# The feed-forward block of a fused transformer kernel: order of the second half's units, w2's sums taken of w2 times g2, another order of the passes, layer norms in pairs

## The chip, the cores and the metric

The kernel runs on one core of a Trainium2 chip. The metric is the device time of one execution in microseconds (us). The core has a matrix engine (PE, whose weight loads have a row of their own, PEld), a vector engine (DVE), an activation engine (ACT), a general engine (POOL) and a queue from which all transfers are issued (SP). Each of them takes its instructions strictly in order and waits at the first one whose inputs or buffers are not ready.

## The reference

A block with differential attention, a gated linear recurrence and a SwiGLU feed-forward layer over 2048 tokens of width 1024, in float32. The change lies in the last part alone:

```python
x = layer_norm(ALPHA * x + g1 * y, ln1_g, ln1_b)
h = modulate(layer_norm(x), sh2, sc2)
a, b = split(h @ w1)                  # w1: 1024 x 2*2816
f = (silu(a) * b) @ w2                # w2: 2816 x 1024
x = layer_norm(ALPHA * x + g2 * f, ln2_g, ln2_b)
```

Here g2 is a vector over the 1024 output columns; it comes from the conditioning vector and is known early.

## The kernel before

A float32 product is made of three products of split numbers: each operand is kept as a rounded part and a rest, and `mm3` issues high times high, high times low and low times high (lines 151 to 153). The split is a cast on ACT and a subtraction, mostly on DVE.

Both products of the feed-forward layer are cut into 2x2 blocks and computed with Strassen's scheme in Winograd's form: seven passes in place of eight, on sums of blocks. S1 to S4 are the sums of the left operand's blocks A11 to A22, T1 to T4 those of the right operand's blocks B11 to B22; `OPS` names the two operands of each pass.

**First product (lines 1040 to 1400).** A `Unit(tb, j)` computes one 128-wide chunk j (of 22) of the hidden layer for two of the four token blocks: group tb=0 is blocks 0 and 1, tb=1 is blocks 2 and 3. It has seven passes of 12 matmuls. For each pass `prep` splits a piece of w1; the sums of w1's blocks are made on POOL (lines 1062 to 1067) out of tiles that SP loads. `fin` takes each pass's sum out of PSUM, mostly on DVE; line 1122 is one addition on POOL in each unit. `put` stores the hidden tile to `hid_d`. The 44 units run in the order tb=0, j=0 to 21, then tb=1, j=0 to 21. Split pieces of w1 rotate over 11 buffers, in the last two units over 7; PSUM has 8 banks.

Two further things are made beside the units:

- The left sums of the second product. They need A11, A12 (group 0, j below 11 and from 11 on) and A21, A22 (group 1, likewise). As soon as `put` has a hidden tile of group 1 with j of 11 or more, it loads three tiles (`qA`), makes S1 and S3 on POOL (lines 1087, 1088) and S2 and S4 on DVE (1089, 1090), and stores four tiles to `sum_d` (`S_d` in the trace). That falls in the last 11 units.
- The right sums, `w2_sums(j)` for j=0 to 10: four loads of w2, four operations on POOL (lines 1373 to 1376), four stores to `t_d` (`T_d`). They are written after units 6 to 16.

Both take their tiles from one pool, `qp`, with six buffers that are used in rotation.

**Second product (lines 1400 to 1525).** Seven passes of eight token tiles each; step n = 8*pass + i. Each step has 33 matmuls and reads a left tile that `load_hid` has loaded and split (line 1431: pieces m=0, 1, 2 on DVE or POOL), and the pass's right operand, which `prep_w2` loads and splits ahead (lines 1413, 1414). The order of the passes is 1, 2, 6, 7, 5, 3, 4. Output tile ti (of 16) has two halves of 512 columns; half 0 of tiles 0 to 7 is complete after pass 2, half 1 of tiles 8 to 15 after pass 5, half 1 of tiles 0 to 7 after pass 3, half 0 of tiles 8 to 15 after pass 4. `evict` adds the PSUM bank to the accumulators, and for a complete half `final` follows on DVE:

```python
V.tensor_tensor(o, o, g2b[:, c], ALU.mult)                       # L1460
V.scalar_tensor_tensor(y, y, ALPHA, o, ALU.mult, ALU.add)        # L1461
V.bn_stats(stt[:, ti, hf, :], y)                                 # L1462
```

A tile's first half is stored to `y0_d`. With its second half the whole layer norm follows at once: the statistics and seven small instructions for the root, two scalings on ACT (L1475), two multiplications by `lg` on POOL (L1476), two additions of `lb` (L1477, one on DVE, one on POOL), two stores. So the norms of tiles 0 to 7 lie in the sixth pass and those of tiles 8 to 15 in the seventh.

What sets the order: a scheduler takes the program in the order in which it is written, and moves instructions on each engine ahead of others by times that it assumes. On the chip that order is fixed.

Of the kernel before, what the change touches and what calls it, by code (L numbers as in the profile page):

```python
# [19 lines left out]
P = 128  # L20
D = 1024
# [29 lines left out]
PASSES = ((1, "A11", "B11"), (2, "A12", "B21"), (6, "S2", "T2"), (7, "S3", "T3"), (5, "S1", "T1"), (3, "S4", "B22"),  # L51
# [14 lines left out]
def kernel(ctx: ExitStack, tc: tile.TileContext, x, cx, prm_d, wa1, wa2, b_ada, w_in, w_v, lqk,  # L66
# [7 lines left out]
    def dma(o, i):  # L74
# [16 lines left out]
           for n in ("T1", "T2", "T3", "T4")}  # L91
    hid_d = [dram.tile([4, P, NJ, P], F32, tag=f"hid{b}", name=f"hid_d{b}") for b in range(NB)]
    y0_d = [dram.tile([P, 512], F32, tag=f"y0{i}", name=f"y0_d{i}") for i in range(16)]
# [950 lines left out]
    class Unit:  # L1044
# [29 lines left out]
        def put(self, s, o):  # L1074
            col = lambda d, j: d[:, :, j, :].rearrange("i p t -> p i t")
            row = lambda t: t.rearrange("p (i t) -> p i t", t=P)
            dma(col(hid_d[2 * self.tb + s], self.j), row(o))
            j = self.j - NJ // 2
            if self.tb == 0 or j < 0:
                return  # L1080

            a = {}
            for n, (b, jj) in (("A21", (2 + s, j)), ("A11", (s, j)), ("A12", (s, self.j))):
                a[n] = qp.tile([P, 512], F32, tag="q", name="q" + n)
                dma(row(a[n]), col(hid_d[b], jj))
            s1 = qp.tile([P, 512], F32, tag="q", name="qS1")
            G.tensor_tensor(s1, a["A21"], o, ALU.add)  # L1087
            G.tensor_tensor(a["A21"], a["A11"], a["A21"], ALU.subtract)  # L1088
            V.tensor_tensor(a["A11"], s1, a["A11"], ALU.subtract)
            V.tensor_tensor(a["A12"], a["A12"], a["A11"], ALU.subtract)  # L1090
            for n, t in (("S1", s1), ("S3", a["A21"]), ("S2", a["A11"]), ("S4", a["A12"])):
                dma(col(sum_d[n][s], j), row(t))

# [76 lines left out]
    units = [Unit(tb, j) for tb in range(2) for j in range(NJ)]  # L1170
# [193 lines left out]
    ahead(2)  # L1364
    def w2_sums(j):

        q = {}
# [12 lines left out]
    for n, u in enumerate(units[6:NJ - 1]):  # L1380
        whole(u, std)
        if n < NJ // 2:
            w2_sums(n)
# [32 lines left out]
    def load_hid(n, q):  # L1416
# [8 lines left out]
        for r in range(2 - q):  # L1425
# [5 lines left out]
            (G if m == 1 or (m == 0 and p > 4) else V).tensor_tensor(t[:, 1], raw[:, 4 * r:4 * r + w],  # L1431
# [14 lines left out]
    g2b = lnp.tile([P, D], F32, tag="g2b", name="g2b")  # L1446
# [139 lines left out]
```

## Time and profile before

| | us |
|---|---|
| Time, median of 3 runs | 2931.16 (2929.72 to 2933.06) |
| The profiled execution's own time | 2931.16 |
| Its span from the first to the last instruction | 2929.3 |
| First product, roughly | 1560 to 2460 |
| Second product, first to last matmul | 2460 to 2894 |
| After the last matmul | 35.3 |

Times within the span are counted from its start. The profile gives for each engine how long it was busy, and for each instruction what released it where the engine had been idle. A matmul of the two products starts every 0.226 us when nothing holds it, 443 in 100 us, so that a stretch with fewer shows how much PE lost there. The granted clock of PE is 1.00 (2.4 GHz) in most stretches and 0.5 (1.2 GHz) for some us after a long pause.

### The profile page before, as it was taken

How to read it: one execution, taken by the hardware profiler on the slowest of the kernel's cores; microseconds unless marked ns; L12 is line 12 of the kernel's file. 1: busy time of each engine (PE TensorE's matmuls, PEld its weight loads, DVE VectorE, ACT ScalarE, POOL GpSimd, SP SyncE). 2: the span in 40 equal slices, each digit the busy share in tenths (PEclk: the TensorE clock that was granted, in tenths of full speed). 3: DMA queues.
4: the chain of work that ended last, by engine and by line, in shares of the span. 5: the costliest groups of instructions: out<-in, count | busy, mean ns of one | idle time of the engine just before them, and what ended most of it. 6: DMA issues, size and time to landing. Idle time of an engine off the chain costs nothing. (4 is left out here: it accounts for less than half of the span.)

```text
span 2929.3 us, 37944 instructions
## 1 busy us (share of the span) xinstructions
PE 2728.2 (93%) x13188; PEld 2270.8 (78%) x13188; DVE 2140.4 (73%) x3399; ACT 1431.0 (49%) x2056; POOL 1559.1 (53%) x1019
## 2 busy tenths in 40 slices
PE   8889889878999999999999899999999988999994
PEld 4868767767899999987777787887888876888873
DVE  7754796596898999995888866758656657544688
ACT  3546668653677777774235433334333223433332
POOL 2004544454788888871454788445545655211376
PEclk9999999989999999999999999999999999999997
DMA  8875537357132322217463476333324888855543
GB/s 326 305 232 175 200 107 273 121 182 221 38 76 76 76 69 60 65 62 255 137 236 109 159 236 218 101 87 91 112 86 123 246 253 273 272 161 167 193 170 128
DMA packets 328848, 474.32 MB, mean 162 GB/s; under 512 B 26056, under 2 KB 201288, under 8 KB 326096
## 3 DMA queue, kind: packets, MB, share of 16 engines
q1 hardware_dynamic: 328656, 471.90, 50.0%
q8 instruction: 104, 1.70, 0.2%
q14 instruction: 88, 0.72, 0.1%
HBM read 313.46 MB, written 158.35 MB: 161 GB/s over the span
## 5 line engine op out<-in xcount | busy, mean ns | idle before, releaser
L857 DVE TENSOR_SCALAR_CACHE_REDUCE e<-ps_s 128x768 f32<-128x768 f32 x384 | 359.5, 951 | 37.3 <-PE ps_s L855 30.0
L873 POOL TENSOR_TENSOR a<-e,e 128x768 f32<-128x768 f32 x192 | 349.3, 1848 | 18.5 <-PE pt L936 13.8
L855 PE MATMUL ps_s<-k,q 128*128 128x384 f32 x1536 | 336.7, 351 | 13.2 <-DVE e L857 11.9
L862 ACT ACTIVATE e<-e,nm 128x2304 f32<-128x2304 f32 x128 | 285.4, 2229 | 52.3 <-DVE nm L861 49.2
L855 PEld LDWEIGHTS ps_s<-k,q 128*128 128x128 f32 x1536 | 268.7, 192 | 28.4 <-DVE e L857 21.4
L1431 POOL TENSOR_TENSOR hid<-hf,hid 128x512 fp32r<-128x512 f32 x72 | 100.4, 1396 | 245.1 <-ACT hid L1430 240.2
L940 ACT CAST ah<-pt 128x512 fp32r<-128x512 f32 x288 | 165.9, 582 | 130.0 <-PE pt L936 127.2
L941 DVE TENSOR_TENSOR al<-pt,ah 128x512 fp32r<-128x512 f32 x288 | 195.9, 686 | 36.1 <-ACT ah L940 35.7
L870 POOL TENSOR_SCALAR e<-e,rr,rn 128x2304 f32<-128x2304 f32 x64 | 146.6, 2291 | 90.2 <-DVE nm L861 48.9
L1062 POOL TENSOR_TENSOR s<-w1r 128x512 f32<-128x512 f32 x44 | 59.5, 1353 | 226.8 <-DMA w1r<-in_w 204.0
L151 PE MATMUL ps_p<-ht,w 128*128 128x512 f32 (+1 forms) x416 | 162.9, 392 | 16.6 <-DVE kf L213 11.6
L936 PE MATMUL pt<-ident,a 128*128 128x128 f32 x1152 | 175.3, 275 | 3.0 <-POOL a L873 2.8
L936 PEld LDWEIGHTS pt<-ident,a 128*128 128x128 f32 x1152 | 144.8, 142 | 42.8 <-POOL a L873 3.7
L153 PE MATMUL ps_p<-ht,w 128*128 128x512 f32 (+1 forms) x416 | 162.2, 392 | 6.6 <-DVE w L183 6.5
L1430 ACT CAST hid<-hf 128x512 fp32r<-128x512 f32 x168 | 95.7, 582 | 148.3 <-PE ps L153 133.1
L152 PE MATMUL ps_p<-ht,w 128*128 128x512 f32 (+1 forms) x416 | 162.3, 390 | 0.0
L219 POOL TENSOR_TENSOR lo<-kf,hi 128x512 fp32r<-128x512 f32 (+1 forms) x36 | 58.8, 1635 | 177.5 <-ACT hi L218 140.6
L929 PE MATMUL po<-ah,v 128*128 128x512 f32 x288 | 126.7, 440 | 0.6 <-ACT ah L940 0.6
L1122 POOL TENSOR_TENSOR v<-v,q 128x512 f32<-128x512 f32 x44 | 68.1, 1549 | 99.4 <-DVE u L1121 99.4
L930 PE MATMUL po<-al,v 128*128 128x512 f32 x288 | 116.8, 405 | 3.1 <-DVE al L941 1.4
L931 PE MATMUL po<-ah,v 128*128 128x512 f32 x288 | 114.7, 398 | 0.0
L151 PEld LDWEIGHTS ps_p<-ht,w 128*128 128x128 f32 x416 | 80.6, 194 | 36.1 <-issue 12.2
(3365 smaller groups left out, 8493.7 us busy)
## 6 DMA issues: line engine op xcount, KB each, us to landing
w1r<-in_w SPq DMA_DIRECT2D x88, 512.0 KB, 4.1
hid_d<-hid SPq DMA_DIRECT2D x88, 256.0 KB, 2.7
qA<-hid_d SPq DMA_DIRECT2D x66, 256.0 KB, 3.7
S_d<-qA SPq DMA_DIRECT2D x66, 256.0 KB, 5.9
wraw<-in_w_in SPq DMA_DIRECT2D x32, 512.0 KB, 4.6
adaw<-in_wa SPq DMA_DIRECT2D x32, 512.0 KB, 4.7
q<-q_d SPq DMA_DIRECT2D x64, 256.0 KB, 4.8
oy<-oy_d SPq DMA_DIRECT2D x16, 1024.0 KB, 5.8
```

The source lines that it names most:

```text
L151: PE.matmul(ps, lhsT=lh, rhs=rh, start=start, stop=False)
L152: PE.matmul(ps, lhsT=lh, rhs=rl, start=False, stop=False)
L153: last["pe"] = PE.matmul(ps, lhsT=ll, rhs=rh, start=False, stop=stop).ins
L855: PE.matmul(ps[:, j, :384], lhsT=q[:, m, part, qt * P:(qt + 1) * P], rhs=kst[h, m][:, c0:c0 + 384], start=(part == 0), stop=(part == 1))
L857: V.tensor_scalar(et[:, cc * 768:(cc + 1) * 768].rearrange("p (a b) -> p a b", a=2), ps[:, :, :384], -0.125, None, ALU.mult, ALU.min, accu ...
L862: S.activation(et, et, AF.Exp, bias=nm[:, m:m + 1], scale=-1.0, accum_out=ss[m])
L870: G.tensor_scalar(es[1], es[1], rr, rn, ALU.mult, ALU.mult)
L873: last["a"] = G.tensor_tensor(a, es[0][:, g * 768:(g + 1) * 768], es[1][:, g * 768:(g + 1) * 768], ALU.add).ins
L929: PE.matmul(po, lhsT=vh, rhs=ah, start=(j == 0), stop=False)
L936: PE.transpose(pt[:, qt * P:(qt + 1) * P], ath[h, b, qt, j // 6][:, (j % 6) * P:(j % 6 + 1) * P], ident)
L940: S.copy(ah, pt)
L941: V.tensor_tensor(al, pt, ah.bitcast(F32), ALU.subtract)
```

## The change

1. The units of the second group run in pairs: j=0, 11, 1, 12, and so on. `put` makes S3 (now as A11 - A21) when the tile of the first half is there, and S1, S2, S4 at the second half's tile: four loads and four stores for each j and block in place of three and four, spread over 22 units in place of 11. S1 and S2 are on POOL, S3 and S4 on DVE. S1, S2 and S3 overwrite tiles that were loaded, so that a put takes one or three buffers in place of four.
2. `g2_row` makes g2 as a row on all partitions and stores it to `g2_d`. `w2_sums(j)` is written after units 10 to 20; it loads two tiles of g2 as well, multiplies the four tiles of w2 by them on DVE, stores three of the products (`B11`, `B22`, `B21`) and makes the four sums as before on POOL. So it has six loads, four DVE and four POOL operations and seven stores, and takes seven buffers of the six in rotation. `prep_w2` always reads from `t_d`, and L1460 is gone.
3. The passes run 1, 2, 6, 5, 3, 7, 4: tiles 0 to 7 are complete after the fifth pass, half 1 of tiles 8 to 15 after the sixth, half 0 after the seventh.
4. `final` stores every half (but one) to `y_d`. `complete` does the norm later, for two tiles at once with one root, from halves that it loads again: tiles 0 to 7 at steps 35, 39, 43 and 47, tiles 8 to 14 at steps 50, 52 and 54, and tile 15 at the end with four fused operations on DVE. From the fifth pass on (before: the sixth) POOL makes piece m=0 of line 1431 too.

```diff
-PASSES = ((1, "A11", "B11"), (2, "A12", "B21"), (6, "S2", "T2"), (7, "S3", "T3"), (5, "S1", "T1"), (3, "S4", "B22"),
+PASSES = ((1, "A11", "B11"), (2, "A12", "B21"), (6, "S2", "T2"), (5, "S1", "T1"), (3, "S4", "B22"), (7, "S3", "T3"),
...
-            j = self.j - NJ // 2
-            if self.tb == 0 or j < 0:
+            if self.tb == 0:
                 return
...
+            a11 = load("A11", hid_d[s], j)
+            if j == self.j:
+                V.tensor_tensor(a11, a11, o, ALU.subtract)
+                return store("S3", a11)
+            a21, a12 = load("A21", hid_d[2 + s], j), load("A12", hid_d[s], self.j)
+            G.tensor_tensor(a21, a21, o, ALU.add)
+            store("S1", a21)
+            G.tensor_tensor(a11, a21, a11, ALU.subtract)
+            store("S2", a11)
+            V.tensor_tensor(a12, a12, a11, ALU.subtract)
+            store("S4", a12)
...
-    units = [Unit(tb, j) for tb in range(2) for j in range(NJ)]
+    units = [Unit(0, j) for j in range(NJ)] + [Unit(1, j + h * (NJ // 2)) for j in range(NJ // 2) for h in range(2)]
...
+        for c in range(2):
+            g.append(qp.tile([P, 512], F32, tag="q", name="g2"))
+            dma(g[c], g2_d[:, c * 512:(c + 1) * 512])
         for n, (r, c) in (("B11", (0, 0)), ("B12", (0, 1)), ("B22", (1, 1)), ("B21", (1, 0))):
...
             dma(q[n], w2[jj * P:(jj + 1) * P, c * 512:(c + 1) * 512])
+            V.tensor_tensor(q[n], q[n], g[c], ALU.mult)
+            if n != "B12":
+                dma(t_d[n][j], q[n])
+        G.tensor_tensor(q["B11"], q["B12"], q["B11"], ALU.subtract)
         t2 = qp.tile([P, 512], F32, tag="q", name="wT2")
-        G.tensor_tensor(q["B11"], q["B12"], q["B11"], ALU.subtract)
...
-            (G if m == 1 or (m == 0 and p > 4) else V).tensor_tensor(t[:, 1], raw[:, 4 * r:4 * r + w],
+            (G if m == 1 or (m == 0 and p > 3) else V).tensor_tensor(t[:, 1], raw[:, 4 * r:4 * r + w],
...
-        V.tensor_tensor(o, o, g2b[:, c], ALU.mult)
         V.scalar_tensor_tensor(y, y, ALPHA, o, ALU.mult, ALU.add)
         V.bn_stats(stt[:, ti, hf, :], y)
...
+        dma(y_d[ti][:, hf], y)
+
+    def complete(tis, y=None):
...
+                if ti == 15:
+                    V.scalar_tensor_tensor(t, t, mv[:, 0, k:k + 1], lg[:, c], ALU.subtract, ALU.mult)
+                    V.scalar_tensor_tensor(t, t, rs[:, k:k + 1], lb[:, c], ALU.mult, ALU.add)
+                else:
+                    S.activation(t, t, AF.Identity, bias=nb[:, k:k + 1], scale=rs[:, k:k + 1])
+                    G.tensor_tensor(t, t, lg[:, c], ALU.mult)
+                    (G if hf else V).tensor_tensor(t, t, lb[:, c], ALU.add)
...
+    norms = {35: (0, 1), 39: (2, 3), 43: (4, 5), 47: (6, 7), 50: (8, 9), 52: (10, 11), 54: (12, 13, 14)}
```

The order on PE is the same as before. On SP, in the middle of w2's sums, there stands before, from one store of T4 to the next (w1r is a load of w1, hid_d a store of a hidden tile):

```order
L75 DMA T4_d2_131<-wB21_16606 128x512
L75 DMA wB21_16766<-in_w2 128x512
L75 DMA w1r_16472<-in_w1 128x1024
L75 DMA T1_d3_99<-wB11_16760 128x512
L75 DMA T2_d3_110<-wT2_16768 128x512
L75 DMA wB11_16920<-in_w2 128x512
L75 DMA T3_d3_121<-wB12_16762 128x512
L75 DMA wB12_16922<-in_w2 128x512
L75 DMA wB22_16924<-in_w2 128x512
L75 DMA T4_d3_132<-wB21_16766 128x512
```

Now, from the store of T4 of j=3 on:

```order
L75 DMA T4_d3_165<-wB21_17426 128x512
L75 DMA wB12_17590<-in_w2 128x512
L75 DMA wB22_17593<-in_w2 128x512
L75 DMA wB21_17597<-in_w2 128x512
L75 DMA B11_d4_100<-wB11_17586 128x512
L75 DMA w1r_16770<-in_w1 128x1024
L75 DMA B22_d4_122<-wB22_17593 128x512
L75 DMA B21_d4_111<-wB21_17597 128x512
L75 DMA T1_d4_133<-wB11_17586 128x512
L75 DMA g2_17753<-g2_d_173 128x512
L75 DMA T2_d4_144<-wT2_17602 128x512
L75 DMA g2_17755<-g2_d_173 128x512
```

The loads of g2 and the stores of B11, B22 and B21 have come in. From the first T4 to the last (ten sums) there stood 11 loads of w1, two to a unit, and now there stand 15.

On POOL, in the last units of the first product, there stands before (s are sums of w1, v and q the units' own additions, qS and qA the left sums):

```order
L1087 TENSOR_TENSOR qS_20619<-qA_20613,hid 128x512
L1088 TENSOR_TENSOR qA_20613<-qA_20615,qA_20613 128x512
L1062 TENSOR_TENSOR s_20877<-w1r 128x512
L1063 TENSOR_TENSOR s_20878<-s_20877,w1r 128x512
L1087 TENSOR_TENSOR qS_20655<-qA_20649,hid 128x512
L1088 TENSOR_TENSOR qA_20649<-qA_20651,qA_20649 128x512
L1122 TENSOR_TENSOR v<-v,q 128x512
L1067 TENSOR_TENSOR s_20878<-w1r,s_20878 128x512
L1123 TENSOR_TENSOR q<-u,q 128x512
L1065 TENSOR_TENSOR s_20877<-w1r 128x512
```

Now, over one unit without left sums and the beginning of the next one with them:

```order
L1063 TENSOR_TENSOR s_19906<-w1r 128x512
L1064 TENSOR_TENSOR s_19907<-s_19906,w1r 128x512
L1132 TENSOR_TENSOR v<-v,q 128x512
L1068 TENSOR_TENSOR s_19907<-w1r,s_19907 128x512
L1133 TENSOR_TENSOR q<-u,q 128x512
L1066 TENSOR_TENSOR s_19906<-w1r 128x512
L1097 TENSOR_TENSOR qA_19823<-qA_19823,hid 128x512
L1099 TENSOR_TENSOR qA_19821<-qA_19823,qA_19821 128x512
L1097 TENSOR_TENSOR qA_19856<-qA_19856,hid 128x512
L1099 TENSOR_TENSOR qA_19854<-qA_19856,qA_19854 128x512
L1063 TENSOR_TENSOR s_20057<-w1r 128x512
L1064 TENSOR_TENSOR s_20058<-s_20057,w1r 128x512
```

Each unit had four operations for the left sums; now every second one has four.

On DVE, at the last two output tiles, there stands before (f takes the PSUM bank, mv to nb are the norm's statistics and root):

```order
L1500 TENSOR_TENSOR f_25858<-acc,ps 128x512
L1460 TENSOR_TENSOR f_25858<-f_25858,g2b 128x512
L1461 SCALAR_TENSOR_TENSOR y<-y,f_25858 128x512
L1477 TENSOR_TENSOR y<-y,lb_22282 128x512
L1462 BN_STATS stt<-y 128x6
L1469 BN_AGGR mv_25867<-stt 128x2
L132 TENSOR_SCALAR rs_a<-mv_25867 128x1
L134 RECIPROCAL rs_y<-rs_y 128x1
L135 TENSOR_TENSOR rs_t<-rs_a,rs_y 128x1
L136 TENSOR_TENSOR rs_t<-rs_t,rs_y 128x1
```

Now, from the last bank's f on:

```order
L1524 TENSOR_TENSOR f_25965<-acc,ps 128x512
L1506 TENSOR_TENSOR y_25919<-y_25919,lb_22470 128x512
L1477 SCALAR_TENSOR_TENSOR y<-y,f_25965 128x512
L1478 BN_STATS stt<-y 128x6
L1488 BN_AGGR mv<-stt 128x2
L133 TENSOR_SCALAR rs_a<-mv 128x1
L1501 SCALAR_TENSOR_TENSOR y<-y,mv,lg_22469 128x512
L1501 SCALAR_TENSOR_TENSOR y_25988<-y_25988,mv,lg_22469 128x512
L135 RECIPROCAL rs_y<-rs_y 128x1
L136 TENSOR_TENSOR rs_t<-rs_a,rs_y 128x1
L137 TENSOR_TENSOR rs_t<-rs_t,rs_y 128x1
L138 TENSOR_SCALAR rs_t<-rs_t 128x1
```

The addition of `lb` to tile 14 (y_25919) now stands between the last bank's f and its scaled addition, and the multiplication by `lg` of the last tile has come before the root.

## Rows read from the trace of the kernel before

**Rows 1.** The page's head: span and instructions.

```profile
span 2929.3 us, 37944 instructions
```

**Rows 2.** Windows: stretch, PE, PEld, DVE, ACT, POOL busy (count), clock, DMA, GB/s.

```profile
1667.00:1802.00 135.00, 129.98 (x574) 106.54 (x573) 93.10 (x88) 41.31 (x74) 123.14 (x82) 1.00 0.77 252
1740.00:1820.00 80.00, 74.64 (x325) 60.35 (x324) 53.94 (x54) 23.45 (x43) 71.47 (x48) 1.00 0.72 241
1860.00:1960.00 100.00, 100.00 (x443) 82.79 (x442) 63.52 (x78) 35.16 (x59) 44.77 (x32) 1.00 0.31 90
2370.00:2470.00 100.00, 81.08 (x329) 62.79 (x328) 65.07 (x82) 28.64 (x53) 51.43 (x37) 0.93 0.89 268
...
2818.00:2842.00 24.00, 17.06 (x59) 12.71 (x58) 21.30 (x36) 9.63 (x18) 16.84 (x12) 0.79 0.52 173
2842.00:2894.00 52.00, 49.81 (x218) 40.28 (x216) 44.97 (x72) 15.44 (x30) 41.68 (x28) 1.00 0.45 155
```

**Rows 3.** PE's longest wait, 2380 to 2520: us in total, times, longest.

```profile
PE ps L153 <- DVE w__21783 L1072: 6.7, 1, 6.7
```

**Rows 4.** Timeline of the longest wait: start, us, operation, [idle before <-releaser].

```profile
2409.81 1.26 POOL L1087 TENSOR_TENSOR qS<-qA,hid 128x512 f32<-128x512 f32 x1 [8.45 <-DMA S_d<-qA]
...
2413.55 1.73 DVE L1089 TENSOR_TENSOR qA<-qS,qA 128x512 f32<-128x512 f32 x1 [8.93 <-POOL qA L1088]
...
2415.80 0.67 DVE L1072 TENSOR_TENSOR w__21783<-w1r,w__21783 128x512 fp32r<-128x512 f32 x1
...
2416.53 0.79 PE L153 MATMUL ps<-B,w__21783 128*128 128x512 f32 x1 [6.71 <-DVE w__21783 L1072]
```

**Rows 5.** Windows of L1122 alone (one per unit): stretch, busy (count), clock, DMA.

```profile
1671.00:1809.00 138.00, 8.22 (x6) 1.00 0.76 249
2107.00:2240.00 133.00, 11.98 (x7) 1.00 0.29 83
2262.00:2416.00 154.00, 10.91 (x7) 0.99 0.86 246
```

**Rows 6.** Transfers 1667 to 1802: count, size, median us to landing.

```profile
wB<-in_w SPq DMA_DIRECT2D x44, 256.0 KB, 4.4
T_d<-wB SPq DMA_DIRECT2D x32, 256.0 KB, 4.5
```

**Rows 7.** Groups of the second product: count, busy us, mean ns, idle before.

```profile
L1461 DVE SCALAR_TENSOR_TENSOR y<-y,f 128x512 f32<-128x512 f32 x32 | 38.7, 1208 | 0.7
L1431 DVE TENSOR_TENSOR hid<-hf,hid 128x384 fp32r<-128x384 f32 x56 | 37.0, 663 | 14.9 <-ACT hid L1430 14.9
...
L1460 DVE TENSOR_TENSOR f<-f,g2b 128x512 f32<-128x512 f32 x32 | 25.2, 788 | 0.4
L1475 ACT ACTIVATE y<-y,nb,rs_y 128x512 f32<-128x512 f32 x32 | 24.3, 808 | 26.2 <-DVE nb L1472 23.7 <-DMA out<-y 2.5
L1462 DVE BATCH_NORM_STATS2 stt<-y 128x6 f32<-128x512 f32 x32 | 22.0, 688 | 0.5
...
L1495 DVE TENSOR_TENSOR f<-ps,acc 128x512 f32<-128x512 f32 x16 | 11.0, 685 | 16.9 <-PE ps L153 16.9
```

**Rows 8.** Timeline of POOL over one tile of the seventh pass.

```profile
2880.21 3.06 POOL L1476 TENSOR_TENSOR y<-y,lg 128x512 f32<-128x512 f32 x2 [1.18 <-ACT y L1475]
...
2889.91 3.07 POOL L1476 TENSOR_TENSOR y<-y,lg 128x512 f32<-128x512 f32 x2 [1.19 <-ACT y L1475]
```

**Rows 9.** Timeline of the end: the last matmul, and DVE's last additions.

```profile
2893.63 0.39 PE L153 MATMUL ps<-w__25210,hid 128*128 128x512 f32 x1
...
2917.87 1.74 DVE L1477 TENSOR_TENSOR y<-y,lb 128x512 f32<-128x512 f32 x1 [1.15 <-POOL y L1476]
...
2924.41 1.63 DVE L1477 TENSOR_TENSOR y<-y,lb 128x512 f32<-128x512 f32 x1
```

**Rows 10.** Transfers of the output halves in the second product: median us to landing.

```profile
y_d<-y SPq DMA_DIRECT2D x16, 256.0 KB, 2.7
...
y<-y_d SPq DMA_DIRECT2D x13, 256.0 KB, 3.1
```

More of the change, by code (lines that the diff above doesn't have):

```diff
@@ L90 @@
     t_d = {n: [dram.tile([P, 512], F32, tag=f"{n}{j}", name=f"{n}_d{j}") for j in range(NJ // 2)]
-           for n in ("T1", "T2", "T3", "T4")}
+           for n in ("B11", "B21", "B22", "T1", "T2", "T3", "T4")}
+    g2_d = dram.tile([P, D], F32, tag="g2", name="g2_d")
     hid_d = [dram.tile([4, P, NJ, P], F32, tag=f"hid{b}", name=f"hid_d{b}") for b in range(NB)]
-    y0_d = [dram.tile([P, 512], F32, tag=f"y0{i}", name=f"y0_d{i}") for i in range(16)]
+    y_d = [dram.tile([P, 2, 512], F32, tag=f"y{i}", name=f"y_d{i}") for i in range(16)]
     wo_d = [dram.tile([P, 2, D], F32R, tag=f"wo{k}", name=f"wo_d{k}") for k in range(8)]
@@ L1077, in put, with load, store @@
             dma(col(hid_d[2 * self.tb + s], self.j), row(o))
-            j = self.j - NJ // 2
-            if self.tb == 0 or j < 0:
+            if self.tb == 0:
                 return
[L1082 to L1091, printed above, removed]
-                dma(col(sum_d[n][s], j), row(t))
+            j = self.j % (NJ // 2)
+            def load(n, d, j):
+                t = qp.tile([P, 512], F32, tag="q", name="q" + n)
+                dma(row(t), col(d, j))
+                return t
+            def store(n, t):
+                dma(col(sum_d[n][s], j), row(t))
+            a11 = load("A11", hid_d[s], j)
[9 more added lines that the diff above has]
+            store("S4", a12)
         def mms(self, p, ks, first, last_):
@@ L1378, in w2_sums @@
             dma(t_d[n][j], t)
-    for n, u in enumerate(units[6:NJ - 1]):
+    for u in units[6:10]:
         whole(u, std)
-        if n < NJ // 2:
-            w2_sums(n)
+    g2_row()
+    for n, u in enumerate(units[10:NJ - 1]):
+        whole(u, std)
+        w2_sums(n)
     sliced(units[NJ - 1], std, range(4), lambda k: build(1, k))
@@ L1473, in final @@
-        for a, t in ((1 - hf, y0), (hf, y)):
-            ca = slice(a * 512, (a + 1) * 512)
-            S.activation(t, t, AF.Identity, bias=nb, scale=rs)
-            (V if ti == 15 else G).tensor_tensor(t, t, lg[:, ca], ALU.mult)
-            (V if a == hf else G).tensor_tensor(t, t, lb[:, ca], ALU.add)
-            dma(out[ti * P:(ti + 1) * P, ca], t)
+        if ti == 15 and hf == 0:
+            return y
+        dma(y_d[ti][:, hf], y)
+    def complete(tis, y=None):
+        mv = sm.tile([P, 2, 4], F32, tag="mv", name="mv", bufs=4)
+        n = len(tis)
+        for k, ti in enumerate(tis):
+            V.bn_aggr(mv[:, :, k], stt[:, ti])
+        rs = rsqrt(mv[:, 1, :n], n, LN_EPS)
+        nb = sm.tile([P, 2], F32, tag="nb2", name="nb2")[:, :n]
+        V.scalar_tensor_tensor(nb, mv[:, 0, :n], -1.0, rs, ALU.mult, ALU.mult)
+        for k, ti in enumerate(tis):
+            for hf in range(2):
+                c = slice(hf * 512, (hf + 1) * 512)
+                if y is None or hf:
+                    t = tile2("y5")
+                    dma(t, y_d[ti][:, hf])
+                else:
+                    t = y
+                if ti == 15:
+                    V.scalar_tensor_tensor(t, t, mv[:, 0, k:k + 1], lg[:, c], ALU.subtract, ALU.mult)
+                    V.scalar_tensor_tensor(t, t, rs[:, k:k + 1], lb[:, c], ALU.mult, ALU.add)
+                else:
+                    S.activation(t, t, AF.Identity, bias=nb[:, k:k + 1], scale=rs[:, k:k + 1])
+                    G.tensor_tensor(t, t, lg[:, c], ALU.mult)
+                    (G if hf else V).tensor_tensor(t, t, lb[:, c], ALU.add)
+                dma(out[ti * P:(ti + 1) * P, c], t)
@@ L1489, in evict @@
             V.tensor_tensor(u, ps, u, ALU.add)
[L1490 removed]
+        elif num == 5:
             V.tensor_tensor(t, ps, u, ALU.add)
@@ L1520 @@
                     mm3(ps, h[:, 0, j % 4], h[:, 1, j % 4], w[:, 0], w[:, 1], j == 0, j == HJ - 1)
-        evict(PASSES[p][0], i, pss[n])
+        y = evict(PASSES[p][0], i, pss[n])
+        if n in norms:
+            complete(norms[n][:2])
+            for ti in norms[n][2:]:
+                complete([ti])
+    complete([15], y)
     s5.close()
```

52 lines of the change are left out of this document (17 added, 35 removed).

## The prediction

> **What bounds the kernel now.** I read four views in this order: the windows, for the stretches in which PE does not run at its pace; PE's waits there; the timeline around the longest of them; and the timeline of the end. The sum is made against the profiled execution, whose span is 2929.3 us [rows 1]; its own time, 2931.16 us, is also the median of the three runs, so 1.9 us are added at the end.
>
> In the feed-forward layer PE is the bound wherever nothing goes wrong: 443 matmuls in 100 us, one in 0.226 us [rows 2]. A unit of 84 matmuls then takes 19.0 us, a step of 33 takes 7.45 us. A stretch's loss is the count that is missing at that pace (some per cent of records can be missing from a trace, so I take a us off in mind, not in the sum). There are four losses that the change can touch:
> - 1740 to 1820, beside w2's sums: 325 matmuls for 354, 6.6 us [rows 2].
> - 2370 to 2470, the end of the first product: 329 for 443, 25.7 us [rows 2].
> - 2818 to 2842: 59 for 106, 10.7 us; 2842 to 2894: 218 for 230, 2.8 us; together 13.5 us [rows 2].
> - After the last matmul, which ends at 2894.0, the span goes on for 35.3 us [rows 1, 9].
>
> The second of these is a chain: PE waits 6.7 us for a split piece of w1 [rows 3], and much the same once more a unit later; that piece waits on DVE behind S2, which waits 8.9 us for POOL, which has itself stood 8.5 us at S1, waiting for the tile that was loaded into a buffer of the ring after a store [rows 4]. The cause lies earlier. POOL's one addition per unit comes every 133/7 = 19.0 us in a quiet stretch, but every 154/7 = 22.0 us when the left sums are made, with transfers at a share of 0.86 in place of 0.29 [rows 5]. DVE and POOL fall 3 us behind in each of 11 units, and PE lives on its lead until it is used up.
>
> **The left sums (part 1 of the change).** The work per j and block rises from seven transfers to eight, POOL's and DVE's operations stay at two each. But it is spread over 22 units in place of 11: eight transfers per unit in place of 14. So the left sums took 0.57 of the transfers' time; 8/14 of that gives 0.29 + 0.33 = 0.62. POOL has two such operations per unit in place of four. With a third of the transfers' time free and little over half the buffers' traffic, I see no reason for the 3 us per unit to go on. The put's transfers are still issued on SP among w1's loads, so a wait there can still hold a load, and the last two units still have few buffers for split pieces: of the 25.7 us I leave 5.7 and take **-20**. Bounds: -25 (nothing left) and -5 (the in-order waits on loaded tiles matter more than the share).
>
> **w2's sums (part 2).** Three things are added. Four DVE multiplications per j, 44 in all: the trace of before has no such operation there; the nearest is a DVE operation of the same stretch, 93.1/88 = 1.06 us [rows 2], so 4.2 us per j. Five more transfers per j. And a longer ring, which I think decides. The six buffers now serve seven tiles, and T4 is made in the place of B21, whose store must have left first. So from one T4 store to the next there lie, one after the other: T4's store (4.5), the load of the next B21 (4.4), its multiplication (1.06), the store of B21 (4.5), the operation for T4 on POOL, 123.1/82 = 1.5 us [rows 2, 6]. That is 16.0 us; with 1.2 us for turns in three queues (an estimate, less than one operation in each) **17.2 us per j**. SP's order has 15 loads of w1, 7.5 units, over ten such cycles: 142 us at PE's pace against 172. So DVE and POOL fall 30 us behind. DVE's own work there, 14 operations per unit before and 5.3 more, is 19.3 x 1.06 = 20.5 us per unit, less than the 22.9 that the ring gives, so the ring is the later of the two.
>
> How much of that reaches PE is read from before: six units took 138 us in place of 114 [rows 5], 24 us late, and PE lost 6.6 of them; the lead covers 17.4 us. So PE loses 30 - 17.4 = 12.1 us with unrounded figures, 5.5 more than before: **+5.5**. Bounds: -6.6, if the cycle stays under 14.2 us and nothing is lost, and +28 at 19.5 us per j. Behind a DVE that waits for a tile of w2 stand the evictions of PSUM and the splits of w1; behind an SP that waits for a store stand the loads of w1. That is how it gets to PE.
>
> The Trainium skill speaks against this term (DMA: Bandwidth & Descriptors, section "Anatomy of one DMA — SWDGE (gpsimd) path"): a transfer costs about 2.0 us plus its bytes at 436 GB/s. By that an estimate for 256 KB is 2.6 us, the cycle would be 11.6 us and nothing would be lost; the transfers of this stretch took 4.4 and 4.5 us [rows 6], so the rule's price is not met here.
>
> The row of g2 itself is six transfers and two POOL operations once, off PE's path behind the lead. The sums now end later, but seven units before the second group's right operands are built; at 19 us a unit the lag is made up by then. I cost both at nothing; if that cover is gone, the build's loss grows by a few us, which is inside the upper bound.
>
> **The second product (parts 2 to 4).** Removed from DVE: 32 multiplications of 0.79 us [rows 7], which lay in all output passes, and seven of 16 roots. But where nothing was late, that is worth nothing: PE runs at 443 in 100 us until the sixth pass. What is late there is POOL. In the last two passes each tile has two multiplications, one addition and two splits on POOL, and a tile takes 9.7 us, from 2880.21 to 2889.91, where PE needs 7.45 [rows 8]. Sixteen tiles give 16 x 2.25 = 36 us that PE's lead, PE's stall (13.5) and the tail must take.
>
> Now the sixteen norms lie over the last three passes, eight of them in 16 steps. Per four steps of the fifth and sixth pass POOL has eight splits and six operations of a norm: 14 x 1.5 = 21 us of 29.8. DVE has per step of the sixth pass two sums from PSUM (0.69 each), the scaled addition (1.21), statistics (0.69) and a split (0.66) [rows 7], 15.7 us in four steps; two additions of `lb`, 3.5 [rows 9]; a root, 1.7 (what the 4.8 us from 2919.6 to 2924.4 leave beside statistics, a scaling of 0.81 and two multiplications of 0.79) [rows 7, 9]; and 5.5 splits of w2 at the 1.06 from above, 5.8: 26.7 us of 29.8. In the seventh pass POOL has 14 splits and 21 operations, 53 us of 59.6. Close, but below. Of the 13.5 us I leave 2: **-11.5**. Bounds: -13.5 and 0.
>
> **The end.** The last norm no longer waits behind a tile that is 9.7 us long. But the fixed order on DVE puts the addition of `lb` to tile 14 before the last tile's scaled addition, and tile 14 has to go out and come back first. Count from the last matmul's end, T. Tile 14's step ends at T - 7.45; an addition of `lb` with its wait for POOL (1.15 + 1.74) [rows 9], the sum (0.69) and the scaled addition (1.21) [rows 7] follow: T - 2.7. Store 2.7 and load 3.1 [rows 10]: T + 3.1. ACT 0.81, POOL 1.53 [rows 7, 8], the addition of `lb` 1.74: T + 7.2. Then tile 15: scaled addition 1.21, statistics 0.69, two fused operations like it (2.42), the root 1.7, two more (2.42): T + 15.6. From DVE's last end, 2926.0, to the span's end there are 3.3 us [rows 1, 9]. So 18.9 us in place of 35.3: **-16.5**. Bounds: -24 (tile 14 in time, so that T + 0.7 replaces T + 7.2 and a us more goes) and -8 (DVE and POOL one tile of 9.7 us late).
>
> **Sum.** 5.5 - 20 - 11.5 - 16.5 = -42.5: a span of 2886.8, a time of **2889 us** with the 1.9. With each term's bounds, not all at the same end, this case reaches from 2877 to 2902.
>
> **The rivals.**
> 1. The ring does not bind: transfers land in the 2.7 to 3.1 us of the second product [rows 10], 11 us a cycle, below 14.2. Then -6.6 in place of 5.5: 2877 us. For it: fewer other transfers per unit there. Against it: 13 transfers a j in place of eight. The Trainium skill's price (DMA: Bandwidth & Descriptors, the section named above) would lead here too.
> 2. The ring binds harder: transfers grow by 0.8 us each under the added traffic, 19.5 us a cycle. 195 - 142.5 - 17.4 = 35 us lost, +28.5: 2912 us.
> 3. **Slower than before**, the same mechanism taken further. It eats the other three terms (48) from 54.6 us lost, which is 72 us behind, 21.5 us a cycle. At 23.5 us it loses 75 us: 2952 us. For it speaks that DVE, POOL and SP are all in order and that each holds a wait of that ring among work for PE; against it, that before's four operations per j, with POOL busy 123 of 135 us, cost no more than 24 us of lag.
> 4. The norms' lag stays: the fuller sixth pass (26.7 of 29.8 us by mean durations) falls behind when more of DVE's operations take the 1.7 us of [rows 9]. Then stall and tail give back 9 together: 2908 us.
> 5. The left sums stay a wait though they are thinner (-5 in place of -20): 2904 us. In 4 and 5 a part of the change doesn't do what it says.
>
> **How the numbers follow.** Chances: the forecast 0.45, rival 1 0.15, rival 2 0.13, rival 3 0.06, rival 4 0.11, rival 5 0.10. The range 2868 to 2915 holds the forecast's own range, rivals 1, 2, 4 and 5 with their spread, and leaves out rival 3 and the outer sides of 1 and 2. About 0.2%, 6 us, is what a measurement of this kernel can tell from no change. Faster by more: 0.91, all but rival 3 and the far end of 2 with 4 and 5 together; slower by more: 0.05; between: 0.04.
>
> **What would show it.** In the windows of the changed kernel: the last 100 us of the first product with over 415 matmuls (left sums), and L1132, the unit's addition on POOL, every 19 us there. Over w2's sums, the time from one T4 operation (L1403) to the next near 17 us, and some 12 us of PE's loss there. No wait of PE over 2 us at the change from the sixth to the seventh pass. Some 19 us after the last matmul. The forecast is wrong if w2's sums cost PE over 40 us, or if a put still holds POOL for a transfer as it did at 2409.81.

## The result, and the profile after

| | before | changed |
|---|---|---|
| Median of 4 runs each, us | 2932.11 | 2895.72 (2890.26 to 2897.33) |
| Ratio, 95% interval | | 0.9874 (0.9856 to 0.9891) |
| Span of the profiled execution, us | 2929.3 | 2892.3 |

The change makes the kernel 36.4 us faster; the forecast was 42 us. The page of the changed kernel begins:

```profile
span 2892.3 us, 38110 instructions
```

Windows of the changed kernel, with the columns of [rows 2]: w2's sums, the end of the first product with the first steps of the second, and the passes of the norms.

```profile
1660.00:1960.00 300.00, 281.34 (x1204) 227.38 (x1203) 231.44 (x251) 93.45 (x168) 204.32 (x136) 0.98 0.68 219
...
2360.00:2560.00 200.00, 200.00 (x884) 165.62 (x883) 120.96 (x155) 76.14 (x133) 75.04 (x51) 1.00 0.72 224
...
2660.00:2760.00 100.00, 98.58 (x436) 81.29 (x435) 59.23 (x86) 40.13 (x69) 59.63 (x42) 1.00 0.65 211
2760.00:2860.00 100.00, 100.00 (x443) 82.79 (x442) 72.94 (x107) 34.67 (x62) 61.38 (x42) 1.00 0.71 239
```

The same two long stretches in the kernel before:

```profile
1660.00:1960.00 300.00, 291.86 (x1284) 240.24 (x1283) 201.22 (x220) 103.00 (x180) 205.97 (x141) 0.99 0.55 172
2360.00:2560.00 200.00, 181.08 (x770) 145.62 (x769) 123.06 (x165) 68.01 (x125) 85.69 (x61) 0.97 0.86 269
```

At 443 matmuls in 100 us, 1329 fit into 300 us. The changed kernel lacks 125 of them, 28.3 us, where the one before lacks 45, 10.2 us: w2's sums cost **18.1 us more**. The other three losses are all but gone. So the sum of the prediction reads, term by term:

| us | forecast | measured | from |
|---|---|---|---|
| w2's sums | +5.5 | +18.1 | 1204 matmuls for 1284 |
| end of the first product | -20 | -25.7 | the 329 of [rows 2] against a full rate |
| second product | -11.5 | -11.9 | 13.5 against the 7 missing from 2660 to 2760 |
| after the last matmul | -16.5 | -14.9 | 35.3 against 20.4 (the last one ends at 2871.9, below) |
| sum | -42.5 | -34.4 | span: -37.0 |

Of the 2.6 us that the last line lacks, about 1 lies in the build of the second group's right operands and in the second product (table below). The rest lies ahead of w2's sums, where the first unit's addition on POOL already comes 3.2 us earlier (1587.7 for 1590.9).

The left sums look as forecast. In the window of POOL's one addition per unit, nine of them take 171 us, 19.0 each, with transfers at 0.68 (forecast 0.62; [rows 5] had 22.0 at 0.86):

```profile
2266.00:2437.00 171.00, 14.61 (x9) 1.00 0.68 202
```

Under w2's sums the same addition (first fence: one took 31 us, the next eight 186.9) and T4's operation (second fence) show two cadences:

```profile
1665.00:1696.00 31.00, 1.77 (x1) 1.00 0.84 269
1696.00:1882.90 186.90, 12.07 (x8) 0.96 0.79 259
```

```profile
1697.00:1871.00 174.00, 15.19 (x10) 0.96 0.78 257
```

Ten T4 in 174 us are 17.4 us a cycle, where 17.2 was forecast. Yet this agreement is an accident, as the transfers of the same stretch show (count, size, median us to landing):

```profile
wB<-in_w SPq DMA_DIRECT2D x39, 256.0 KB, 3.4
B_d<-wB SPq DMA_DIRECT2D x30, 256.0 KB, 2.6
...
T_d<-wB SPq DMA_DIRECT2D x29, 256.0 KB, 4.0
```

With these the ring's chain is 4.0 + 3.4 + 1.1 + 2.6 + 1.5 = 12.6 us, 13.8 with the 1.2 us for turns. It is shorter than 14.2, so by the prediction's own reckoning it does not bind, and PE should have lost nothing, as rival 1 has it. It lost 28.3 us. The Trainium skill (DMA: Bandwidth & Descriptors, "Anatomy of one DMA — SWDGE (gpsimd) path") has 2.0 us plus the bytes at 436 GB/s for a transfer that POOL issues. Taken over to these, which SP issues, that is an estimate of 2.6 us for 256 KB; the stores of B landed in just that, the loads and the stores of T shown here did not.

DVE shows another candidate: its multiplications by g2, in the groups of DVE from 1700 to 1880 (count, busy us, mean ns, idle us just before them):

```profile
L1396 DVE TENSOR_TENSOR wB<-wB,g 128x512 f32<-128x512 f32 x40 | 43.1, 1082 | 20.8 <-DMA wB<-in_w 16.4 <-issue 4.3
```

The mean of 1.08 us was forecast (1.06). The 20.8 us in which DVE stands at loads that were issued shortly ahead were not.

The end, from the timelines of the changed kernel:

```profile
2871.49 0.39 PE L154 MATMUL ps<-w__25326,hid 128*128 128x512 f32 x1
...
2872.92 1.73 DVE L1506 TENSOR_TENSOR y<-y,lb 128x512 f32<-128x512 f32 x1 [0.95 <-POOL y L1505]
...
2877.50 0.68 DVE L1524 TENSOR_TENSOR f<-acc,ps 128x512 f32<-128x512 f32 x1
...
2880.89 1.73 DVE L1506 TENSOR_TENSOR y<-y,lb 128x512 f32<-128x512 f32 x1 [2.71 <-POOL y L1505]
...
2882.15 1.59 POOL L1506 TENSOR_TENSOR y<-y,lb 128x512 f32<-128x512 f32 x1
2882.54 1.75 DVE L1477 SCALAR_TENSOR_TENSOR y<-y,f 128x512 f32<-128x512 f32 x1
...
2885.37 1.41 DVE L1501 SCALAR_TENSOR_TENSOR y<-y,mv,lg 128x512 f32<-128x512 f32 x2
...
2887.73 1.41 DVE L1502 SCALAR_TENSOR_TENSOR y<-y,rs_y,lb 128x512 f32<-128x512 f32 x2
```

### The profile page after: what moved, and what is told of

Its sections match the earlier page's. It is cut to its first block, busy times and chain, and to the rows that moved or that the text cites. A ratio compares the mean times of both kernels' runs of the same rounds, so it can differ in the third digit from the quotient of the medians.

```text
span 2892.3 us, 38110 instructions
## 1 busy us (share of the span) xinstructions
PE 2717.0 (94%) x13188; PEld 2264.2 (78%) x13188; DVE 2163.7 (75%) x3355; ACT 1429.4 (49%) x2047; POOL 1584.7 (55%) x1027
## 4 chain that ended last, share of the span: by engine, by line
PE 54%; DVE 10%; DMA 6%; POOL 4%; issue 4%; ACT 3%; SPq 1%; DVEq 0%; ACTq 0%; POOLq 0%
PE ps L153 10%; PE ps L154 10%; PE ps L152 10%; PE ps_s L856 8%; PE pt L937 4%; PE po L931 2%; PE po L932 2%; PE po L930 2%; DMA wB<-in_w 1%; DVE e L858 1%; PE ps_w L1261 1%; DMA w1r<-in_w 1%; PE ps_w L1265 1%; PE ps_w L1262 1%; PE ps_l L1261 1%
## 5 line engine op out<-in xcount | busy, mean ns | idle before, releaser
L858 DVE TENSOR_SCALAR_CACHE_REDUCE e<-ps_s 128x768 f32<-128x768 f32 x384 | 359.6, 952 | 36.8 <-PE ps_s L856 28.3
L1453 POOL TENSOR_TENSOR hid<-hf,hid 128x512 fp32r<-128x512 f32 x80 | 113.2, 1422 | 240.0 <-ACT hid L1452 240.0
```

The source lines that it names most:

```text
L858: V.tensor_scalar(et[:, cc * 768:(cc + 1) * 768].rearrange("p (a b) -> p a b", a=2), ps[:, :, :384], -0.125, None, ALU.mult, ALU.min, accu ...
```

## Experiments: undoing one part at a time

The table holds for all experiments: lost us by matmuls missing at 443 in 100 us, 0.226 us each (from the profiled execution; some tenths are uncertain), the time after the last matmul, and the median.

| | w2's sums 1660-1960 | build 1960-2060 | 2360-2560 | 2560 to last matmul | after it | median |
|---|---|---|---|---|---|---|
| before | 10.2 | 9.5 | 26.2 | 15.1 | 35.3 | 2932.1 |
| changed | 28.3 | 8.8 | 0.5 | 2.9 | 20.4 | 2895.7 |
| old_left | 29.4 | 9.3 | 28.3 | 6.6 | 21.4 | 2928.3 |
| old_norms | 31.2 | 8.6 | 0.5 | 13.0 | 30.5 | 2919.1 |
| y_ring | 29.4 | 9.5 | 0.5 | 18.7 | 18.0 | 2913.9 |
| no_w2g2 | 11.8 | 8.8 | 0.5 | 20.4 | 26.1 | 2903.6 |
| no_mult | 6.8 | 8.6 | 0.5 | 7.3 | 21.9 | 2879.2 |
| free_mult | 20.1 | 8.6 | 0.2 | 3.4 | 21.8 | 2890.6 |
| t4_own | 35.7 | 7.9 | 0.5 | 7.7 | 19.8 | 2908.6 |
| spread | 18.5 | 36.2 | 0.5 | 3.4 | 23.8 | 2918.7 |
| paced | 0 | 23.3 | 0.2 | 5.9 | 20.8 | 2885.3 |
| best_a | 6.3 | 11.8 | 0.5 | 7.1 | 19.0 | 2879.0 |
| best_b | 6.3 | 12.0 | 0.5 | 3.0 | 22.2 | 2881.8 |
| best_d | 1.8 | 21.9 | 0.5 | 5.0 | 17.0 | 2885.6 |

**old_left**: part 1 of the diff reversed (`put` and the order of the units).

```diff
-    units = [Unit(0, j) for j in range(NJ)] + [Unit(1, j + h * (NJ // 2)) ...]
+    units = [Unit(tb, j) for tb in range(2) for j in range(NJ)]
```

> The changed kernel with part 1 alone undone: unit order and left sums as before. Theory (the left sums in 11 units were the cause of the whole loss at the end of the first product and of the first steps of the second): 2370 to 2470 loses some 25 us again, 2922 us. Rival (the last two units' seven buffers for pieces of w1 hold PE): +5 to +10, 2901 to 2906 us.

Ratio to before 0.9987 (0.9975 to 0.9999), a median of 2928 for the 2922 expected. The loss is back where it was, with transfers at 0.85 and 0.89 in place of 0.72:

```profile
2360.00:2460.00 100.00, 81.44 (x343) 64.60 (x342) 58.05 (x77) 23.01 (x43) 57.00 (x42) 0.96 0.85 247
2460.00:2560.00 100.00, 98.57 (x418) 80.45 (x419) 67.09 (x87) 46.86 (x86) 37.12 (x25) 0.96 0.89 286
```

So the whole loss was that of the left sums as they were made before, in 11 units with four buffers to a put. Which of the two counts, the density or the buffers, this run does not separate. The last two units' few buffers for pieces of w1, for which the forecast left 5.7 us, cost nothing by themselves: with the thin sums 0.5 us is lost.

**old_norms**: parts 3 and 4 reversed; with them the final step's tile `y` comes from the ring of six again, as in the kernel before.

```diff
-PASSES = (..., (6, "S2", "T2"), (5, "S1", "T1"), (3, "S4", "B22"), (7, "S3", "T3"),
+PASSES = (..., (6, "S2", "T2"), (7, "S3", "T3"), (5, "S1", "T1"), (3, "S4", "B22"),
```

> The changed kernel with parts 3 and 4 undone: order of the passes, norms at once and halves in y0 as before, but g2 stays in w2's sums, so that DVE has 32 operations less than before. Theory (POOL's 9.7 us a tile made the stall and the late end): both return, +12 and +15, 2922 us. Rival (DVE's multiplications by g2 were part of the cycle, so that without them a tile takes less): only the end's order costs, +8 to +15, 2904 to 2911 us.

Ratio 0.995 (0.9932 to 0.9968): +23 us on the changed kernel. The stall is back almost in full, 13.0 us for 15.1, without L1460 on DVE: POOL's timeline in the seventh pass has a tile every 9.2 us (2854.13 to 2863.29), where [rows 8] has 9.7 and PE needs 7.45.

```profile
2854.13 2.86 POOL L1494 TENSOR_TENSOR y<-y,lg 128x512 f32<-128x512 f32 x2 [1.57 <-ACT y L1493]
...
2863.29 2.85 POOL L1494 TENSOR_TENSOR y<-y,lg 128x512 f32<-128x512 f32 x2 [1.57 <-ACT y L1493]
```

So the stall goes with POOL's cycle, as the theory says; without the multiplications on DVE a tile takes 0.5 us less than in the kernel before, and the end 5 us less. Two things stay open here: of the 9.2 us POOL waits 1.57 for ACT, and how much of the 23 us is due to `y` in the ring (y_ring, below) was not tried with the old norms.

**no_w2g2**: part 2 reversed; for lack of room the final step's `y` had to come from the ring of six again. The changed kernel gives `y` two buffers of its own, which the four parts of the change ahead do not name.

```diff
+        V.tensor_tensor(o, o, g2b[:, hf * 512:(hf + 1) * 512], ALU.mult)
         V.scalar_tensor_tensor(y, y, ALPHA, o, ALU.mult, ALU.add)
```

> The changed kernel with part 2 alone undone: w2's sums are of plain w2, written after units 6 to 16, and g2 is multiplied in the final step again. Theory (w2's sums with g2 cost PE some 28 us where the old ones cost 10): about 18 us come back in the first product, the 32 multiplications of 0.79 us on DVE lie beside matmuls but for the last two, so +2 at the end: about 2880 us where the changed kernel takes 2896. Rival (the loss in the first product has another cause than w2's sums, or the multiplications make DVE late in the sixth pass again): 2890 to 2900 us.

Ratio 0.9901 (0.9884 to 0.9918). The first product gave its 17 us back, but the second one and the end took 23. **y_ring** separates the two edits in it: the changed kernel with `y` from the ring alone.

```diff
-        y = lnp.tile([P, 512], F32, tag="y", name="y", bufs=2)
+        y = tile2("y")
```

> The changed kernel with one edit: the final step's tile y comes from the ring of six again, as it had to in no_w2g2, where it was taken from the ring for lack of room. Theory (the 26 us which no_w2g2 lost in the second product and at the end come from DVE's multiplications by g2): no difference, 2893 to 2899 us. Rival (they come from the ring, which the norms' reloaded halves share): 2910 to 2922 us.

Ratio 0.9943 (0.9926 to 0.996): 18 us slower than the changed kernel, so the rival holds. ACT's longest wait from 2740 on (us in total, times, longest), in y_ring:

```profile
ACT y L1504 <- DMA y<-y_d: 54.2, 16, 10.3
```

and the same wait in the changed kernel:

```profile
ACT y L1504 <- DMA y<-y_d: 19.8, 8, 4.4
```

With `y` in the ring the halves that the norms load again come late, and ACT, on which the splits of the left tiles stand behind them, with them. So a line of the diff that I had read as a mere renaming is worth 18 us, where part 1 is worth 33 (old_left) and parts 3 and 4 together with this line 23 (old_norms). Against y_ring, no_w2g2 gains 17 us in the first product, and 32 multiplications cost 10 in the second product and at the end; by the medians it is 10 us faster, by the profiled spans 4 (2904.6 for 2908.6). So part 2 taken alone costs some us where `y` lies in the ring. Beside a `y` with buffers of its own it wasn't tried.

## Experiments: what w2's sums wait for

**no_mult** and **free_mult**: without the multiplications, and with 44 of the same size, at about the same places on DVE, on a tile that nothing loads. Both leave g2 out of the result.

```diff
-            V.tensor_tensor(q[n], q[n], g[c], ALU.mult)
+            with tc.issue_after(hist[at[j]]):          # free_mult; no_mult: nothing
+                V.tensor_tensor(dm, dm, dm, ALU.mult)
```

> The changed kernel without the 44 multiplications of w2 by g2 on DVE, so that g2 is left out of the result; loads and stores all stay. Theory 1 (the ring's cycle of 17.3 us is the cause): each cycle gets 1.1 us shorter, DVE and POOL come 12 us less late, 2884 to 2888 us. Theory 2 (DVE's standing at the loads of w2 and its added work are the cause): the loss beside w2's sums falls from 28 to the 10 of before, 2876 to 2880 us. Theory 3 (the added transfers alone): no gain, 2893 us or more.

> The changed kernel where the 44 multiplications of w2 by g2 are replaced by 44 of the same size on a tile that is always there, at the same places among DVE's instructions (g2 is left out of the result). It separates DVE's work from DVE's standing at loads. If the work alone makes DVE late: 2890 to 2896 us, as the changed kernel. If DVE's standing at loads that are issued just before is what costs: 2878 to 2884 us, as no_mult (2879).

Ratios 0.982 (0.9805 to 0.9834) and 0.9856 (0.9837 to 0.9874). The added transfers alone cost nothing (6.8 us lost where before lost 10.2), and the share of transfers from 1660 to 1960 is the same in both, 0.69. DVE's group in free_mult:

```profile
L1404 DVE TENSOR_TENSOR dm<-dm 128x512 f32<-128x512 f32 x38 | 42.3, 1114 | 0.4
```

The same 42 us of work as in the changed kernel, and no standing: 20.1 us are lost. The windows of free_mult and of the changed kernel show how near DVE is to its end:

```profile
1700.00:1880.00 180.00, 168.01 (x725) 136.32 (x724) 161.85 (x154) 49.06 (x90) 148.59 (x94) 0.99 0.80 267
```

```profile
1700.00:1880.00 180.00, 162.97 (x678) 129.56 (x676) 145.18 (x146) 44.99 (x82) 133.08 (x87) 0.96 0.79 259
```

In free_mult DVE works for 161.9 of 180 us. In the changed kernel it works for 145.2 and stands for 20.8 at loads, 166 in all, while PE gets through fewer matmuls (678 for 725). So of the 21.5 us between no_mult and the changed kernel, 13.3 come with DVE's added work at this density, and 8.2 with what binds the multiplications to their loads, DVE's standing among it; by the medians it is 11.4 and 5.1. no_mult's time is that of theory 2, in which work and standing go together; free_mult's is at the low end of work alone. Both causes are there, and the work is the larger.

**t4_own**: a link of the ring's chain taken out.

```diff
-        G.tensor_tensor(q["B21"], t2, q["B21"], ALU.subtract)
+        G.tensor_tensor(g[1], t2, q["B21"], ALU.subtract)
```

> The changed kernel with T4 written over the second tile of g2 in place of B21, so that it need not wait for B21's store; that takes one link of 2.6 to 4.5 us out of the ring's cycle. Theory 1 (ring): the cycle falls to 13 to 14 us, the loss beside w2's sums to under 15, 2880 to 2885 us. Theory 2 (DVE's standing and work): no change, 2892 to 2900 us.

Ratio 0.9919 (0.9901 to 0.9936). Ten T4 now take 196.8 us, 19.7 each, longer rather than shorter:

```profile
1699.00:1895.80 196.80, 16.34 (x10) 0.97 0.74 240
```

The links that are left come to 3.4 + 4.6 + 1.0 + 1.6 = 10.6 us there (store of T4, load, multiplication, T4, from the transfers and operations of this run), so the chain as the prediction sums it does not set this cadence. Both theories had the time wrong. DVE stands longer at its loads, 27.7 us for 20.8 (group from 1699 to 1896); why was not followed:

```profile
L1396 DVE TENSOR_TENSOR wB<-wB,g 128x512 f32<-128x512 f32 x40 | 38.5, 970 | 27.7 <-DMA wB<-in_w 25.1 <-issue 2.5
```

That does not make the ring idle. In no_mult and free_mult, where the loads of w2 took 5.0 us, the links come to 14.9 and 15.6 us, of 15.7 and 16.7 from one T4 to the next. But the ring's lag is not what PE lost: by the prediction's reckoning cadences of 15.7, 16.7 and 17.4 us (changed) would cost 0, 7 and 14 us, and 6.8, 20.1 and 28.3 were lost.

**spread**: each sum's loads tied behind a hidden tile's store, ten sums to 12 units.

```diff
+            with tc.issue_after(last["H"]):
+                w2_sums(at.index(n))
```

> The changed kernel with w2's sums tied to units: each sum's loads are issued behind the hidden tile's store of a unit (7 to 10, 12 to 15, 17 to 19) and g2's row is made after unit 6; ten sums then stand beside 12 units in place of 7.5. Same instructions, same six buffers. Theory (the loss is the time by which DVE and POOL come late, because ten cycles of 17.3 us stand beside 7.5 units of 19.0, plus the start and the end of them, less a lead of 17.4): 12 units take 228 us, the cycles 174, so nothing is lost: 2868 to 2872 us. Rival (each sum costs DVE and SP a wait whatever stands beside it, or the sums now collide with the build of units 20 and 21): 2885 us or more.

Ratio 0.9955 (0.9938 to 0.9972). My theory of this run, by which only the ratio of cycles to units counts, fell. DVE's group from 1760 to 2060:

```profile
L1396 DVE TENSOR_TENSOR wB<-wB,g 128x512 f32<-128x512 f32 x40 | 28.7, 741 | 50.9 <-DMA wB<-in_w 40.8 <-issue 9.9
```

Fewer operations per unit, but DVE stands for 50.9 us in all. The hidden tile's store waits for DVE, the loads of w2 stand behind it on SP, and an instruction of DVE a few places on waits for these loads: a circle from DVE through SP and the transfers back to DVE. At the sum around 2005, the store is issued at 2003.82, the loads from 2005.32 on, and DVE stands for 4.8 us until 2010.40.

**paced**: one sum for every 10 passes, with the multiplications tied behind an eviction of PSUM, and the loads left free, which puts them about a unit ahead.

```diff
+            with tc.issue_after(last["V5"]):
+                V.tensor_tensor(q[n], q[n], g[c], ALU.mult)
...
+        n, r = divmod(next(passes), 10)
+        if r == 0 and n < NJ // 2:
+            w2_sums(n)
```

> The changed kernel with g2's row made earlier and one sum of w2 for every ten passes (1.43 units) from the seventh unit on; the multiplications are tied behind the PSUM eviction of the unit's pass, the loads are not, and come to stand about a unit ahead of them on SP. Unlike spread, where the loads stood behind the unit's hidden tile and the multiplications right behind the loads. Theory 2 (what costs is DVE standing at loads that were issued just before): the loss beside w2's sums falls to under 10 us, 2868 to 2878 us. Rival (stores that wait for the multiplications now hold SP in front of w1's loads): 2890 us or more.

Ratio 0.9843 (0.9829 to 0.9858). Beside the sums nothing is lost any more, and DVE stands for 5.8 us, at nearly the density of spread, where it stood for 50.9 (groups from 1700 to 2000, and two windows):

```profile
L1397 DVE TENSOR_TENSOR wB<-wB,g 128x512 f32<-128x512 f32 x40 | 38.5, 1014 | 5.8 <-DMA wB<-in_w 4.9 <-issue 0.9
```

```profile
1660.00:1960.00 300.00, 299.99 (x1331) 248.49 (x1331) 231.20 (x258) 99.45 (x179) 207.75 (x136) 1.00 0.65 207
1960.00:2060.00 100.00, 84.10 (x340) 64.82 (x339) 84.67 (x104) 41.31 (x74) 55.18 (x38) 0.95 0.50 155
```

But the build that follows loses 23.3 us in place of 8.8, so 10 us of the 28 are gained.

## Experiments: a version that beats both

**best_a** takes paced with 8 passes to a sum, and tile 14's additions of `lb` on POOL; **best_b** also tile 13's, with tile 14's norm behind the last bank; **best_d** is paced one unit earlier with tile 14 as in best_a.

```diff
-        n, r = divmod(next(passes), 10)
+        n, r = divmod(next(passes), 8)                          # best_a, best_b
...
-                    (G if hf else V).tensor_tensor(t, t, lb[:, c], ALU.add)
+                    (G if hf or ti == 14 else V).tensor_tensor(t, t, lb[:, c], ALU.add)   # best_b: ti > 12
...
+    whole(units[5], std, lambda: (late(), paced()))             # best_d
```

> paced with one sum for every eight passes, so that the sums end before unit 19 and not in the build, and with tile 14's addition of lb on POOL for both halves, so that DVE does not stand for POOL between the last bank and its scaled addition. Theory: the 14 us that paced lost more than the changed kernel in the build go, and the time after the last matmul falls from 20 to some 16 us: 2866 to 2872 us. Rival (a sum in 21.7 us is again too fast for the transfers, and DVE stands): 2876 us or more.

> best_a, and also tile 13's additions of lb on POOL, and the norm of tile 14 written behind the last bank's scaled addition, so that its root doesn't hold DVE before it. Theory: the last bank is taken 3 to 5 us earlier and the tail gets shorter by as much: 2862 to 2868 us. Rival (POOL, with two more additions in the last steps, becomes the last, or tile 14's norm now ends after tile 15's): as best_a or up to 4 us more.

> paced with everything of w2's sums one unit earlier (again one sum for every ten passes, from the sixth unit on, so that the last sum ends before unit 20), and tile 14's addition of lb on POOL as in best_a. Theory (paced's 14 us in the build came from its last sum lying there, and best_a's 6 us before the build from 21.7 us for a sum being too fast): neither is lost, the build takes its 9 us, 2885 - 14 - 1 = 2870 us. Rival (the lag is carried into the build whatever the last sum's place): 2880 us or more.

Ratios 0.9818 (0.9801 to 0.9835), 0.9829 (0.981 to 0.9848) and 0.9842 (0.9828 to 0.9855). best_a has the lowest median of all kernels here that compute the whole, at 2879.0 us some 17 us below the changed kernel; its interval overlaps those of the other two, and none of the three came down to what was expected. In best_d the last sum still ended among the first loads of the build, and the build lost 22 us as in paced; whether it is the meeting or a lag carried over is open. At the end of best_a, the timeline has the last scaled addition 7.0 us after the last matmul's end (2858.26), where the changed kernel has it after 10.7, but the finish is not as much earlier:

```profile
2865.22 0.69 DVE L1482 SCALAR_TENSOR_TENSOR y<-y,f 128x512 f32<-128x512 f32 x1
...
2866.35 2.93 POOL L1510 TENSOR_TENSOR y<-y,lg 128x512 f32<-128x512 f32 x2 [2.35 <-ACT y L1509]
2866.99 2.84 DVE L1506 SCALAR_TENSOR_TENSOR y<-y,mv,lg 128x512 f32<-128x512 f32 x2
...
2869.25 2.92 POOL L1511 TENSOR_TENSOR y<-y,lb 128x512 f32<-128x512 f32 x2
...
2872.68 1.41 DVE L1507 SCALAR_TENSOR_TENSOR y<-y,rs_y,lb 128x512 f32<-128x512 f32 x2
```

The pair that multiplies by `lg` takes 2.84 us beside POOL, which now has the additions; in the changed kernel, where POOL is done by then, it takes 1.41 (2885.37, above). The gain at the end is 1.4 us.

## Why the prediction was right where it was, and wrong where it was not

The time lies 6.7 us above the forecast and inside its range. Three terms of four hold within 6 us, and two errors partly cancel. Of the signs that were named, the 443 matmuls at the end of the first product, the 19.0 us between additions, the 17 us between T4s and the 20 us after the last matmul came, and PE's longest wait in the second product is 1.4 us; PE's loss beside w2's sums was 28 us in place of 12.

- **What bounds the kernel.** Held: four losses were named, and all else of the span moved by some 2.6 us. The first was counted from 1740 on, as 6.6 us; from 1660 on it was 10.2.
- **The left sums**, -20 for -25.7. The mechanism held (cadence 19.0, old_left), as far as old_left tells thinner sums from fewer buffers. The 5.7 us that were left for the in-order waits and the few buffers were not needed.
- **w2's sums**, +5.5 for +18.1: mis-sized, by two steps. The first is "so the ring is the later of the two": I took the larger of the ring's 22.9 us and DVE's 20.5 us per unit, and let the ring decide. free_mult between no_mult and the changed kernel shows DVE's work and its standing to decide, and t4_own that the chain as summed does not; on an engine that takes its instructions in order, work and waits add up where the larger was taken. The second is "at nothing": the start and the end of the sums were put behind the lead that had already been spent on their middle. Nine units, not 7.5, came late: 31 and 187 us for nine additions in place of 171, 47 us. Less the lead of 17.4 that is 29.5 us, and 28.3 were measured. The lead, read from the kernel before, fits. That the ring's cycle came out at 17.4 us for 17.2 was luck: its links were 12.6.
- **Removed from DVE: "where nothing was late, that is worth nothing".** Wrong by some 10 us where `y` lies in the ring: there, no_w2g2 against y_ring, the 32 multiplications cost that much in the second product and at the end. With `y` in buffers of its own no run shows it.
- **The second product**, -11.5 for -11.9. Right, but for a reason that was incomplete: y_ring shows 16 us of loss here that only `y`'s own two buffers keep away, and the prediction did not price them.
- **The end**, -16.5 for -14.9. The chain was the right one. Its `lb` step was put at T + 5.5 and came at T + 9.0, since tile 13's addition and tile 14's root (2872.92 to 2877.50) kept DVE before the last bank and POOL was late for tile 14 (2.71 us).
- **The rivals.** 1 had the ring's links nearly right (12.6 us for its 11), and was wrong that PE then loses nothing. 2 had the sums at +28.5 and 3 higher still, by the ring, which did not decide. 4 and 5 did not come.

## What to carry to other kernels

When instructions are added to an engine that works in order beside the bound one, add its work and its waits; don't take the larger. Put loads into the program a full stage ahead of the instruction that needs them, and tie that instruction, not the load, to its place: the same 40 multiplications cost 5.8 us of standing so (and in fewer per unit), 20.8 where the scheduler had put them, and 50.9 where the loads stood behind a store that waits for the same engine. A lead can be spent once, so count all that comes late from the first such unit to the last; and look at which buffers a diff gives to what, even where it seems to rename only.

## What the runs showed of the hardware

DVE's durations depend on POOL: the same pair of instructions took 1.41 and 2.84 us (above), and an instruction on 128x1 elements 1.18 and 0.16 us in the roots of the changed kernel's last two tiles, with POOL at work and without:

```profile
2874.06 2.93 POOL L1506 TENSOR_TENSOR y<-y,lb 128x512 f32<-128x512 f32 x2
...
2875.82 1.18 DVE L137 TENSOR_TENSOR rs_t<-rs_t,rs_y 128x1 f32<-128x1 f32 x1
...
2887.07 0.16 DVE L137 TENSOR_TENSOR rs_t<-rs_t,rs_y 128x1 f32<-128x1 f32 x1
```

The Trainium skill says why (SBUF — State Buffer, "SBUF: two separate sides"): a DVE operation with two inputs in this memory and an operation of POOL that reads it lock each other out for a whole instruction. The rows here agree in kind; the wait appears as a longer duration and not as idle time, so a DVE that seems busy may be standing. I had used means, 1.06 us, which hold this waiting as long as POOL's load stays as it is.
